# Pre-norm scales from sums gathered before the residual add, half of the residual update inside the state-space pipeline, and the direct term of that pipeline in its tables

## The chip, the cores and the metric

The kernel runs on one core of a Trainium2 chip. The metric is the device time of one execution in microseconds, the median of several runs. The engines are TensorE (PE; its weight loads PEld), VectorE (DVE), ScalarE (ACT), GpSimd (POOL) and SyncE (SP, which issues the DMA transfers).

## The reference

One inference step of a two-layer hybrid decoder over T = 576 positions (512 of a prompt, 8 sequences of 8 more) and a model width of 1024. Six sub-layers follow each other: feed-forward, S5 state-space mixer with GLU, feed-forward; feed-forward, multi-head latent attention, feed-forward. Each is wrapped in two norms:

```
x += w * RMSNorm_post(f(RMSNorm_pre(x)))        # w is 1/2 for the feed-forwards
rms_norm(x, g) = x * rsqrt(mean(x*x) + 1e-6) * g
swiglu(x)      = (silu(x @ w_gate) * (x @ w_up)) @ w_down          # inner width 2816
s5_mixer(u):   s_t = A s_(t-1) + B u_t (complex, 64 groups of 16 channels, 64 states)
               y = Re(C s) + d * u
               z = gelu(y) @ w_glu ; out = z[:1024] * sigmoid(z[1024:])
```

The other part of the reference, the attention with its projections and cache, is not touched by the change.

## The kernel before, in words

The residual stream X lies in SBUF as 8 blocks of 128 channels by 576 positions; the positions are worked in two halves of 288 (h = 0, 1). Matrix products run as three matmuls each (`mm3`, L156 to L158: high by high, high by low, low by high part), 128x288 per instruction. A block (m, h) below is one output block of 128 channels for one half.

RMS norms need sums over channels, that is over partitions. ScalarE squares each output block (L143), GpSimd adds the squares into ACC (L147), and TensorE multiplies ACC with a column of ones (`stats`, L103: four small matmuls for the four quarters of 72 positions of a half). VectorE makes the reciprocal root in nine small operations (L107 to L116, 72x4) and a diagonal matrix `rs_d` (L119); `spread` (L127) multiplies it with ones, so that every partition holds the scale of each position.

The end of a sub-layer is `tail`: the last two blocks of half 0, `stats` of half 0 (d0), block (6,1), then `post` for half 0 (L209: t = Y * g * scale; L211: X += t, partly on GpSimd; L153: split of X * g into high and low part, ACT and DVE), block (7,1), and two pending steps for half 1: its `stats` (d1) and its `post`. The pending steps are run inside the next sub-layer's `first_units`, which computes four output tiles of half 0 (96 matmuls), then of half 1 (96). After `post` the squares of the new X are taken and added once more (`squares`), and `first_units` asks for their `stats` and the two spreads into R, the scale of the pre-norm; R multiplies the products only at their evacuation (L313, L315), so the first products don't wait for it.

The state-space stage (`s_u`, `s_a`, `s_b`, ... ) is a software pipeline over k = 0 to 7 (128 channels each): transposes to time-major tiles (L692 or L700), transposes back (L711), input matmuls (L723), products with rotation tables `rt` (L728, L729), a scan with the decay factors (L737), products (L739 on POOL, L740 on DVE), output matmuls (L757, L760), the direct term d * u (L774), the GELU (L775 to L782) and the split (L153). Its tables (WV, RT, CA, KT, MD) are built during the first feed-forward, in pieces, and go through DRAM. Before the loop it takes squares of X half 1 on ScalarE, adds some on VectorE, and makes both scales.

The order of instructions on each engine is fixed when the kernel is built; each engine works its own list in order.

Of the kernel before, what the change touches and what calls it, by code (L numbers as in the profile page):

```python
# [17 lines left out]
T = 576  # L18
# [7 lines left out]
def build(nc, tc, a, subs=(0, 1, 2, 3, 4, 5)):  # L26
# [9 lines left out]
    with ctx:  # L36
# [40 lines left out]
        ACC = cst.tile([128, T], F32, name="ACC")  # L77
        GP = cst.tile([128, 6, 2, 8], F32, name="GP")
# [19 lines left out]
        def stats(accs, col=None, scale=1.0, eps=1e-6):  # L98

            src = psum()[:CP, :4]  # L100
            for i, z in enumerate(accs):
                for j in range(4):
                    P.matmul(src[:, j:j + 1], z[:, j * CP:j * CP + CP], ones[:, 0:1] if col is None else col,  # L103
                             start=i == 0 and j == 0, stop=i == len(accs) - 1 and j == 3)
            q, t, y = [cur["sm"].tile([CP, 4], F32, name=nm) for nm in ("rs_a", "rs_t", "rs_y")]

            V.tensor_scalar(q, src, eps, None, op0=OP.add)  # L107
# [8 lines left out]
            V.scalar_tensor_tensor(y, t, 5.0, y, op0=OP.add, op1=OP.mult)  # L116
            d = smt("rs_d")[:CP]
            state["y"] = y
# [3 lines left out]
            return d  # L122

# [8 lines left out]
        def sqacc(acc, src, first, scale=1.0, defer=False, ve=False, add=None):  # L132
# [6 lines left out]
            if first:  # L139
                A.activation(acc, src, AF.Square, scale=scale)  # L140
                return None
            sq = sqd.tile([128, H], F32, name="sqd") if defer else smt("sq")
            ins = A.activation(sq, src, AF.Square, scale=scale)  # L143
            if defer:
                state["sqd"] = ins
                return sq
            (add or G).tensor_tensor(acc, acc, sq, op=OP.add)  # L147
# [56 lines left out]

        def post(n, h, rs, nxt):
            last = None
            for k in range(8):
                t = smt("t1")
                V.scalar_tensor_tensor(t, Y[:, k, hs(h)], GP[:, n, 1, k:k + 1], rs, op0=OP.mult, op1=OP.mult)  # L209
                ve = k % 2 if nxt in (None, 1) else k % 4 == 0  # L210
                ins = (V if ve else G).tensor_tensor(X[:, k, hs(h)], X[:, k, hs(h)], t, op=OP.add)  # L211
                last = last if ve else ins
                if nxt is None:
                    if k % 2:
                        S.dma_start(a["o_y"][:, k - 1:k + 1, hs(h)], X[:, k - 1:k + 1, hs(h)])
                elif nxt != 1:
                    xsplit(nxt, h, k)
            if nxt == 1 and h == 1:
                state["add"] = last
                s5["D0"] = stats([ACC[:, hs(0)]]), state["y"]  # L220
                sqs = []
                for k in range(8):
                    sqs.append(s5["sq"].tile([128, H], F32, name="sq%d" % k))
                    A.activation(sqs[k], X[:, k, hs(h)], AF.Square)
                for x, y in ((4, 5), (6, 7), (4, 6)):
                    V.tensor_tensor(sqs[x], sqs[x], sqs[y], op=OP.add)
                s5["D1"] = stats(sqs[:5]), state["y"]
            elif h == 1:
                squares(h, nxt, last)
            return last  # L230

        def squares(h, nxt, last):
            if nxt is not None:
                with tc.issue_after(last.ins), tc.issue_after(state["sqd"].ins):
                    for k in range(8):
                        sqacc(ACC[:, hs(h)], X[:, k, hs(h)], k == 0, add=G)

# [1318 lines left out]
```

## Time and profile before

| | us |
|---|---|
| median of 3 runs | 2486.22 (2485.14 to 2488.54) |
| profiled execution, its time | 2486.95 |
| profiled execution, its span | 2485.2 |
| TensorE busy | 2381.8 (96%) |
| VectorE busy | 1281.5 (52%) |
| ScalarE busy | 873.6 (35%) |
| GpSimd busy | 556.1 (22%) |
| mean granted clock of TensorE | 0.978 of 2.4 GHz |

The span is what the profile sees, first to last instruction; the time has 1.8 us around it. Busy shares are averages over stages with different limits. In order of time the stages are: feed-forward (to 458), state-space start and loop (to 583), GLU (to about 690), two feed-forwards (to about 1560), attention (to about 2030), feed-forward.

### The profile page before, as it was taken

How to read it: one execution, taken by the hardware profiler on the slowest of the kernel's cores; microseconds unless marked ns; L12 is line 12 of the kernel's file. 1: busy time of each engine (PE TensorE's matmuls, PEld its weight loads, DVE VectorE, ACT ScalarE, POOL GpSimd, SP SyncE). 2: the span in 40 equal slices, each digit the busy share in tenths (PEclk: the TensorE clock that was granted, in tenths of full speed). 3: DMA queues.
4: the chain of work that ended last, by engine and by line, in shares of the span. 5: the costliest groups of instructions: out<-in, count | busy, mean ns of one | idle time of the engine just before them, and what ended most of it. 6: DMA issues, size and time to landing. Idle time of an engine off the chain costs nothing.

```text
span 2485.2 us, 44160 instructions
## 1 busy us (share of the span) xinstructions
PE 2381.8 (96%) x17610; PEld 2313.1 (93%) x17610; DVE 1281.5 (52%) x2647; ACT 873.6 (35%) x1807; POOL 556.1 (22%) x819
## 2 busy tenths in 40 slices
PE   7999999789989999998999999899999999999998
PEld 7999999679989999998999999798888898999997
DVE  7564565685464233347432433767777655423434
ACT  4222322353332222224222222434666653222221
POOL 3123535452231001124100112530000042100112
PEclk9999999799989999998999999999999999999999
DMA  3224343473212222222223222345555332222221
GB/s 126 86 86 146 126 130 118 125 188 97 77 60 86 71 92 86 75 88 68 80 67 101 86 70 76 114 114 178 169 173 179 130 104 69 75 74 99 86 71 63
DMA packets 114642, 254.89 MB, mean 103 GB/s; under 512 B 25122, under 2 KB 53539, under 8 KB 114179
## 3 DMA queue, kind: packets, MB, share of 16 engines
q1 hardware_dynamic: 114434, 252.06, 32.0%
q8 instruction: 139, 2.28, 0.4%
q14 instruction: 69, 0.56, 0.1%
HBM read 231.79 MB, written 22.59 MB: 102 GB/s over the span
## 4 chain that ended last, share of the span: by engine, by line
PE 68%; DVE 6%; ACT 2%; issue 1%; POOL 1%; DMA 1%; SPq 0%; ACTq 0%; DVEq 0%; POOLq 0%
PE ps L158 20%; PE ps L156 20%; PE ps L157 20%; PE ps L1331 2%; PE ps L1296 2%; DVE XHL L153 1%; DVE t L209 1%; POOL X L211 1%; PE ps L127 1%; PE ps L1237 1%; DVE wlo L151 1%; PE ps L1317 0%; PE ps L757 0%; PE ps L1225 0%; ACT Pm L1198 0%
## 5 line engine op out<-in xcount | busy, mean ns | idle before, releaser
L156 PE MATMUL ps<-XHL,whi 128*128 128x288 f32 x3344 | 1002.4, 300 | 20.4 <-ACT whi L151 12.9
L157 PE MATMUL ps<-XHL,whi 128*128 128x288 f32 x3344 | 998.7, 299 | 4.7 <-DVE XHL L153 4.7
L158 PE MATMUL ps<-XHL,wlo 128*128 128x288 f32 x3344 | 995.9, 298 | 1.4 <-DVE wlo L151 1.4
L156 PEld LDWEIGHTS ps<-XHL,whi 128*128 128x128 f32 x3344 | 638.2, 191 | 24.3 <-ACT whi L151 13.5
L157 PEld LDWEIGHTS ps<-XHL,whi 128*128 128x128 f32 x3344 | 639.0, 191 | 9.6 <-DVE XHL L153 7.4
L158 PEld LDWEIGHTS ps<-XHL,wlo 128*128 128x128 f32 x3344 | 637.9, 191 | 2.2 <-DVE wlo L151 2.0
L151 DVE TENSOR_TENSOR wlo<-raw,whi 128x1024 fp32r<-128x1024 f32 (+2 forms) x349 | 409.3, 1198 | 317.3 <-ACT whi L151 316.6
L151 ACT ACTIVATE whi<-raw 128x1024 fp32r<-128x1024 f32 (+2 forms) x349 | 321.6, 946 | 446.0 <-PE ps L157 378.2
L158 PE MATMUL ps<-HH,wlo 128*128 128x288 f32 x1408 | 415.8, 296 | 1.9 <-DVE wlo L151 1.9
L156 PE MATMUL ps<-HH,whi 128*128 128x288 f32 x1408 | 417.3, 296 | 0.0
L157 PE MATMUL ps<-HL,whi 128*128 128x288 f32 x1408 | 415.3, 295 | 0.0
L316 POOL TENSOR_TENSOR t<-t,t 128x288 f32<-128x288 f32 x176 | 143.1, 813 | 1113.2 <-DVE t L315 983.5
L158 PEld LDWEIGHTS ps<-HH,wlo 128*128 128x128 f32 x1408 | 265.2, 188 | 2.6 <-DVE wlo L151 2.6
L156 PEld LDWEIGHTS ps<-HH,whi 128*128 128x128 f32 x1408 | 265.3, 188 | 0.4
L157 PEld LDWEIGHTS ps<-HL,whi 128*128 128x128 f32 x1408 | 265.3, 188 | 0.2
L315 DVE TENSOR_TENSOR t<-ps,R 128x288 f32<-128x288 f32 x176 | 80.2, 456 | 331.3 <-PE ps L158 331.1
L147 POOL TENSOR_TENSOR ACC<-ACC,sq 128x288 f32<-128x288 f32 x137 | 138.3, 1010 | 391.2 <-ACT sq L143 387.0
L314 ACT ACTIVATE t<-t 128x288 f32<-128x288 f32 x176 | 77.9, 444 | 329.6 <-DVE t L313 313.2
L151 ACT ACTIVATE HH<-t 128x288 fp32r<-128x288 f32 x176 | 77.2, 439 | 249.0 <-POOL t L316 242.2
L151 DVE TENSOR_TENSOR HL<-t,HH 128x288 fp32r<-128x288 f32 x176 | 81.7, 465 | 125.2 <-ACT HH L151 124.8
L313 DVE TENSOR_TENSOR t<-ps,R 128x288 f32<-128x288 f32 x176 | 79.3, 450 | 53.8 <-PE ps L158 47.9
L369 DVE TENSOR_TENSOR Y<-ps,Y 128x288 f32<-128x288 f32 x64 | 29.2, 455 | 129.4 <-PE ps L158 129.4
(332 smaller groups left out, 2612.9 us busy)
## 6 DMA issues: line engine op xcount, KB each, us to landing
raw<-GU SPq DMA_DIRECT2D x176, 512.0 KB, 4.1
pgr<-PG SPq DMA_DIRECT2D x128, 320.0 KB, 3.5
raw<-DN SPq DMA_DIRECT2D x64, 512.0 KB, 3.5
raw<-DN SPq DMA_DIRECT2D x64, 192.0 KB, 3.4
raw<-GLU SPq DMA_DIRECT2D x16, 512.0 KB, 4.2
CAd<-s5w SPq DMA_DIRECT2D x8, 576.0 KB, 3.6
WVd<-s5w SPq DMA_DIRECT2D x8, 512.0 KB, 3.4
wv<-WVd SPq DMA_DIRECT2D x8, 512.0 KB, 5.8
```

The source lines that it names most:

```text
L147: (add or G).tensor_tensor(acc, acc, sq, op=OP.add)
L151: return A.activation(hi, src, AF.Copy), V.tensor_tensor(lo, src, hi.bitcast(F32), op=OP.subtract)
L156: P.matmul(o, wh, xh, start=st, stop=False)
L157: P.matmul(o, wh, xl, start=False, stop=False)
L158: P.matmul(o, wl, xh, start=False, stop=sp)
L313: V.tensor_tensor(t, pp[0], R[:, hs(h)], op=OP.mult)
L314: A.activation(s, t, AF.Silu)
L315: V.tensor_tensor(u, pp[1], R[:, hs(h)], op=OP.mult)
L316: g = G.tensor_tensor(u, u, s, op=OP.mult)
L369: ins = V.tensor_tensor(y, o, y, op=OP.add)
L1296: P.matmul(so, qb[:, cb], d["kv"][u][:, :, 256 + cb * 128:384 + cb * 128], start=cb == 0, stop=False)
L1331: P.matmul(o, d["pt"][:, c], d["kv"][i // 2][:, i % 2, 0:256], start=i == 0, stop=i == 3)
```

## The change

Three things are done.

- For every output block, three sums are gathered instead of one (`ymom`): of Y squared in ACC, of (Y g) X in R, of (Y g) squared in ACQ. ScalarE makes two squares, VectorE one product, GpSimd three adds. `mom_a` sends the six groups of small matmuls (two per sum) and makes the post-norm scale y; `mom_b` computes from the two other sums and the old sum of X squared, kept in SA, the sum of the new X squared: SA + y (2 sum(Y g X) + y sum((Y g)^2)), in six small VectorE operations, and with eight more the pre-norm scale and its diagonal. The squares of the new X after `post` go, and so do the `stats` in `first_units`. The spreads into R are written in `tail` and in its pending step.
- At the state-space stage `post` of half 1 is taken apart: `post1(k)` runs inside the pipeline's step for k, followed by a scaled copy of X on ScalarE. The pre-norm scale enters at the evacuation of the first transposes (eight ACT copies of 72x128 instead of two of 72x512).
- In the loop the direct term d * u is added to the KT table when that is built, the negated rotation and the scan's decay factors come as two more planes of RT (512 KB a step instead of 256), two additions and one product move from GpSimd to VectorE, and the GELU is rewritten with one VectorE instruction less per half.

```diff
+        def mom_a(h, SQ):
+            src = sums([[ACC[:, hs(h)], SQ[h][0]]])
+            bc = sums([[R[:, hs(h)], SQ[h][1]], [ACQ[:, hs(h)], SQ[h][2]]])
+            q = cur["sm"].tile([CP, 4], F32, name="rs_a")
+            V.tensor_scalar(q, src, 1e-6, None, op0=OP.add)
+            y = rsqrt(q)
+            return y, bc
+        def mom_b(h, y, bc):
+            m = cur["sm"].tile([CP, 4], F32, name="rs_m")
+            V.tensor_tensor(m, bc[:, 4:8], y, op=OP.mult)
+            V.scalar_tensor_tensor(m, bc[:, 0:4], 2.0, m, op0=OP.mult, op1=OP.add)
+            V.tensor_tensor(m, m, y, op=OP.mult)
+            V.tensor_tensor(SA[:, h], SA[:, h], m, op=OP.add)
+            V.tensor_scalar(SA[:, h], SA[:, h], 0.0, None, op0=OP.max)
+            q = cur["sm"].tile([CP, 4], F32, name="rs_ab")
+            V.tensor_scalar(q, SA[:, h], 1e-6, None, op0=OP.add)
+            y2 = rsqrt(q, "b")
+            return diag(y2, tag="b"), y2
+        def ymom(n, m, h, y, sc=1.0):
+            g = GP[:, n, 1, m:m + 1]
+            out = []
+            for i, acc in enumerate((ACC, R, ACQ)):
...
+                if i == 1:
+                    V.scalar_tensor_tensor(dst, y, g, X[:, m, hs(h)], op0=OP.mult, op1=OP.mult)
+                else:
+                    A.activation(dst, y, AF.Square, scale=g if i else sc)
+                if 0 < m < 7:
+                    G.tensor_tensor(acc[:, hs(h)], acc[:, hs(h)], dst, op=OP.add)
+                out.append(dst)
+            return out
...
-            d0 = stats([ACC[:, hs(0)], SQ[0]])
+            y0, bc0 = mom_a(0, SQ)
+            d0 = diag(y0)
             blk(mlast[0], 1)
...
-            last = post(n, 0, spread(d0), nxt)
+            post(n, 0, spread(d0), nxt)
             for m in mlast[1:]:
                 blk(m, 1)
-            squares(0, nxt, last)
-            d1 = []
-            state["pend"] = [lambda: d1.append(stats([ACC[:, hs(1)], SQ[1]])), lambda: post(n, 1, spread(d1[0]), nxt)]
+            if nxt == 1:
+                s5["D0"] = mom_b(0, y0, bc0)
...
+                    spread(d1, ACC[:, hs(1)])
+                    s5["post"] = lambda k: post1(n, 1, ACC[:, hs(1)], nxt, k)
...
+            if nxt is not None:
+                spread(mom_b(0, y0, bc0)[0], R[:, hs(0)])
+            z = {}
+            def norm1():
+                z["y"], z["bc"] = mom_a(1, SQ)
+                z["d"] = diag(z["y"])
+            def rest1():
+                post(n, 1, spread(z["d"]), nxt)
+                if nxt is not None:
+                    spread(mom_b(1, z["y"], z["bc"])[0], R[:, hs(1)])
+            state["pend"] = [norm1, rest1]
...
-            d0 = stats([ACC[:, hs(0)]])
...
-                        spread(d0, R[:, hs(0)])
...
-            spread(d1, R[:, hs(1)])
...
-                    V.scalar_tensor_tensor(u, X[:, k], GP[:, n, 0, k:k + 1], R, op0=OP.mult, op1=OP.mult)
+            def scaled(k):
+                s5["post"](k)
+                u = UN[k] = lp.tile([128, T], F32, name="un")
+                for h in range(2):
+                    A.activation(u[:, hs(h)], X[:, k, hs(h)], AF.Copy, scale=GP[:, n, 0, k:k + 1])
...
-                G.tensor_tensor(m1, Z, RT[:, 0:1].to_broadcast([128, 2, 4, 64]), op=OP.mult)
+                V.tensor_tensor(m1, Z, RT[:, 0:1].to_broadcast([128, 2, 4, 64]), op=OP.mult)
...
-                    V.tensor_scalar(w, sq, 0.044715, 1.0, op0=OP.mult, op1=OP.add)
-                    G.tensor_tensor(w, w, y, op=OP.mult)
+                    V.scalar_tensor_tensor(w, sq, 1 / 0.044715, y, op0=OP.add, op1=OP.mult)
```

What this does to the order of instructions is seen at two places, both at the boundary between the second and the third feed-forward. First TensorE's list at the end of block (7,1), the last product of the old sub-layer (HH, HL are its inputs, XHL those of the next sub-layer). Before:

```order
L156 MATMUL ps<-HH,whi 128x288
L157 MATMUL ps<-HL,whi 128x288
L158 MATMUL ps<-HH,wlo 128x288
L156 MATMUL ps<-XHL,whi 128x288
L157 MATMUL ps<-XHL,whi 128x288
L158 MATMUL ps<-XHL,wlo 128x288
```

And the same place of the changed kernel:

```order
L207 MATMUL ps<-HH,whi 128x288
L208 MATMUL ps<-HL,whi 128x288
L209 MATMUL ps<-HH,wlo 128x288
L181 MATMUL ps<-rs_d,ones 128x288
L207 MATMUL ps<-XHL,whi 128x288
L208 MATMUL ps<-XHL,whi 128x288
L209 MATMUL ps<-XHL,wlo 128x288
```

The spread of the pre-norm's half 0 (L181) now stands between the two; before, it came behind 71 of the first products, two stats groups, the spread of d1 and more products. In the changed kernel 12 first products follow it, then the six groups of half 1, 24 products, the spread of d1, 60 products, and the spread of the pre-norm's half 1 ahead of half 1's 96 products. At the boundaries into the attention and behind it the order is the same; into the second feed-forward that spread of half 0 stands there too, and the one of half 1 follows the spread of d1 by 30 products.

Second VectorE's list there, where that spread's diagonal is made (`rs_yb` is the pre-norm's reciprocal root, `rs_d` the diagonal, t and X belong to `post` of half 0). The changed kernel, first where the chain of `mom_b` meets `post`:

```order
L117 SCALAR_TENSOR_TENSOR rs_yb<-rs_tb,rs_yb 72x4
L420 TENSOR_TENSOR Y<-ps,Y 128x288
L118 SCALAR_TENSOR_TENSOR rs_tb<-rs_yb 72x4
L259 SCALAR_TENSOR_TENSOR t_12062<-Y,GP,ps 128x288
L170 SCALAR_TENSOR_TENSOR sq<-Y,GP,X 128x288
```

and, behind 15 further rows of `post` of half 0 and its weight splits, its end:

```order
L204 SCALAR_TENSOR_TENSOR XHL<-X,GP,XHL 128x288 x4
L420 TENSOR_TENSOR Y<-ps,Y 128x288
L119 TENSOR_TENSOR rs_tb<-rs_tb,rs_ab 72x4
L202 TENSOR_TENSOR wlo<-raw,whi 128x1024
L170 SCALAR_TENSOR_TENSOR t_12139<-Y,GP,X 128x288
L120 SCALAR_TENSOR_TENSOR rs_tb<-rs_tb 72x4
L202 TENSOR_TENSOR wlo<-raw,whi 128x1024
L121 SCALAR_TENSOR_TENSOR rs_yb<-rs_tb,rs_yb 72x4
L127 SCALAR_TENSOR_TENSOR rs_d<-ident,rs_yb 72x288
```

Eleven operations of `mom_b` stand in front of `post`, three and the diagonal behind it. Before, the rows at the end of that `post` were these:

```order
L153 SCALAR_TENSOR_TENSOR XHL<-X,GP,XHL 128x288 x4
L369 TENSOR_TENSOR Y<-ps,Y 128x288
L151 TENSOR_TENSOR wlo<-raw,whi 128x1024 x2
L107 TENSOR_SCALAR rs_a<-ps 72x4
L108 TENSOR_SCALAR rs_y<-rs_a 72x4
```

There the chain of d1, the post-norm scale of half 1, followed at once.

## Rows read from the trace of the kernel before

**Rows 1.** The page: busy time of each engine, share, instructions.

```profile
PE 2381.8 (96%) x17610; PEld 2313.1 (93%) x17610; DVE 1281.5 (52%) x2647; ACT 873.6 (35%) x1807; POOL 556.1 (22%) x819
```

**Rows 2.** What TensorE waited for: us in total, times, longest.

```profile
PE ps L127 <- DVE rs_d L119: 35.2, 13, 4.8
```

**Rows 3.** TensorE in order of time, the spreads: start, us, engine, line, operation.

```profile
1109.89 0.65 PE L127 MATMUL ps<-rs_d,ones 72*128 72x288 f32 x2
1130.26 1.14 PE L127 MATMUL ps<-rs_d,ones 72*128 72x288 f32 x2 [1.86 <-DVE rs_d L119]
1146.87 1.30 PE L127 MATMUL ps<-rs_d,ones 72*128 72x288 f32 x2 [3.70 <-DVE rs_d L119]
1159.38 0.65 PE L127 MATMUL ps<-rs_d,ones 72*128 72x288 f32 x2
```

**Rows 4.** TensorE in order of time: a sums group; block (7,1)'s end.

```profile
1104.28 0.29 PE L158 MATMUL ps<-HH,wlo 128*128 128x288 f32 x1
1104.41 0.62 PE L103 MATMUL ps<-ones,ACC 128*72 128x1 f32 x8
1104.89 0.38 PE L156 MATMUL ps<-HH,whi 128*128 128x288 f32 x1
1114.59 0.29 PE L158 MATMUL ps<-HH,wlo 128*128 128x288 f32 x1
```

**Rows 5.** VectorE in order of time, same boundary.

```profile
1106.69 0.16 DVE L107 TENSOR_SCALAR rs_a<-ps 72x4 f32<-72x4 f32 x1 [1.62 <-PE ps L103]
1108.43 0.45 DVE L119 SCALAR_TENSOR_TENSOR rs_d<-ident,rs_y 72x288 f32<-72x288 f32 x1
1110.09 0.46 DVE L369 TENSOR_TENSOR Y<-ps,Y 128x288 f32<-128x288 f32 x1 [1.20 <-PE ps L158]
1122.99 0.44 DVE L369 TENSOR_TENSOR Y<-ps,Y 128x288 f32<-128x288 f32 x1
1123.35 2.34 DVE L151 TENSOR_TENSOR wlo<-raw,whi 128x1024 fp32r<-128x1024 f32 x2
1131.43 0.94 DVE L209 SCALAR_TENSOR_TENSOR t<-Y,GP,ps 128x288 f32<-128x288 f32 x2 [1.23 <-PE ps L127]
1142.19 0.15 DVE L107 TENSOR_SCALAR rs_a<-ps 72x4 f32<-72x4 f32 x1
1145.79 0.94 DVE L119 SCALAR_TENSOR_TENSOR rs_d<-ident,rs_y 72x288 f32<-72x288 f32 x1
```

**Rows 6.** Stretches: length, each engine's busy time, granted clock, DMA share, GB/s.

```profile
1146.50:1149.00 2.50, 2.13 (x7) 1.87 (x8) 0.57 (x2) 0.41 (x1) 0.00 (x0) 0.50 0.00 0
1149.00:1151.50 2.50, 2.50 (x14) 2.50 (x14) 1.66 (x5) 1.22 (x3) 0.95 (x2) 0.61 0.00 0
```

**Rows 7.** State-space loop: a turn's stretch; VectorE's lines; one instruction.

```profile
513.00:523.00 10.00, 8.45 (x88) 6.98 (x88) 9.59 (x19) 5.81 (x17) 5.96 (x7) 1.00 0.92 234
L669 DVE SCALAR_TENSOR_TENSOR un<-X,GP,R 128x576 f32<-128x576 f32 x4 | 5.1, 1285 | 0.0
L774 DVE SCALAR_TENSOR_TENSOR t<-un,s5d,ps 128x288 f32<-128x288 f32 x10 | 4.7, 508 | 1.8 <-PE ps L772 1.8
L778 DVE TENSOR_SCALAR t<-sq 128x288 f32<-128x288 f32 x10 | 7.8, 782 | 1.1 <-ACT sq L775 1.1
L740 DVE TENSOR_TENSOR Y<-Y,rt 128x512 f32<-128x512 f32 x5 | 6.9, 1373 | 0.0
490.93 0.69 DVE L740 TENSOR_TENSOR Y<-Y,rt 128x512 f32<-128x512 f32 x1
```

**Rows 8.** GpSimd's adds in attention's output, then in the first feed-forward's end.

```profile
L147 POOL TENSOR_TENSOR ACC<-ACC,sq 128x288 f32<-128x288 f32 x12 | 11.1, 927 | 85.6 <-ACT sq L143 85.6
L147 POOL TENSOR_TENSOR ACC<-ACC,sq 128x288 f32<-128x288 f32 x12 | 16.4, 1367 | 36.8 <-ACT sq L143 36.8
```

**Rows 9.** TensorE in order of time, start of the state-space stage.

```profile
466.17 1.30 PE L127 MATMUL ps<-rs_d,ones 72*128 72x288 f32 x2 [4.75 <-DVE rs_d L119]
483.94 0.39 PE L723 MATMUL ps<-U,wv 128*64 128x72 f32 x2
```

More of the change, by code (lines that the diff above doesn't have):

```diff
@@ L95, in smt, with sums, rsqrt @@
             return cur["sm"].tile([128, w], dt, name=name, **(dict(bufs={"t1": 4, "sq": 3}[name]) if name in ("t1", "sq") else k))
-        def stats(accs, col=None, scale=1.0, eps=1e-6):
-            src = psum()[:CP, :4]
-            for i, z in enumerate(accs):
+        def sums(groups, col=None):
+            src = psum()[:CP, :4 * len(groups)]
+            lst = [(z, g) for i in range(max(map(len, groups))) for g, q in enumerate(groups) for z in q[i:i + 1]]
+            for i, (z, g) in enumerate(lst):
                 for j in range(4):
[L103 to L107, printed above, removed]
+                    P.matmul(src[:, 4 * g + j:4 * g + j + 1], z[:, j * CP:j * CP + CP], ones[:, 0:1] if col is None else col,
+                             start=i == 0 and j == 0, stop=i == len(lst) - 1 and j == 3)
+            return src
+        def rsqrt(q, tag="a"):
+            t, y = [cur["sm"].tile([CP, 4], F32, name=nm + tag) for nm in ("rs_t", "rs_y")]
             V.tensor_scalar(y.bitcast(I32), q.bitcast(I32), -0.5, float(0x5F1FFFF9), op0=OP.mult, op1=OP.add)
@@ L122, in stats @@
             return d
+        def stats(accs, col=None, scale=1.0, eps=1e-6, keep=None):
+            src = sums([accs], col)
+            q = cur["sm"].tile([CP, 4], F32, name="rs_a")
+            V.tensor_scalar(q, src, eps, None, op0=OP.add)
+            if keep is not None:
+                V.tensor_copy(SA[:, keep], src)
+            return diag(rsqrt(q), scale)
+        def mom_a(h, SQ):
+            src = sums([[ACC[:, hs(h)], SQ[h][0]]])
+            bc = sums([[R[:, hs(h)], SQ[h][1]], [ACQ[:, hs(h)], SQ[h][2]]])
+            q = cur["sm"].tile([CP, 4], F32, name="rs_a")
+            V.tensor_scalar(q, src, 1e-6, None, op0=OP.add)
[16 more added lines that the diff above has]
+            for i, acc in enumerate((ACC, R, ACQ)):
+                dst = acc[:, hs(h)] if m == 0 else (smt("t1") if i else sqd.tile([128, H], F32, name="sqd")) if m == 7 else smt("sq")
+                if i == 1:
[6 more added lines that the diff above has]
+            return out
         def spread(d, out=None):
@@ L130, in spread, with sqacc @@
             A.activation(out, pp, AF.Copy)
-        def sqacc(acc, src, first, scale=1.0, defer=False, ve=False, add=None):
+        def sqacc(acc, src, first, ve=False):
             if ve:
@@ L139, in sqacc @@
             if first:
-                A.activation(acc, src, AF.Square, scale=scale)
+                A.activation(acc, src, AF.Square)
                 return None
[L142 to L147, printed above, removed]
+            sq = smt("sq")
+            A.activation(sq, src, AF.Square)
+            G.tensor_tensor(acc, acc, sq, op=OP.add)
         def split(hi, lo, src, g=None):
@@ L203, in xsq, with post1 @@
                     sqacc(ACC[:, hs(h)], X[:, k, hs(h)], k == 0, ve=True)
+        def post1(n, h, rs, nxt, k):
+            t = smt("t1")
+            V.scalar_tensor_tensor(t, Y[:, k, hs(h)], GP[:, n, 1, k:k + 1], rs, op0=OP.mult, op1=OP.mult)
+            ve = k % 2 if nxt in (None, 1) else k % 4 == 0
+            (V if ve else G).tensor_tensor(X[:, k, hs(h)], X[:, k, hs(h)], t, op=OP.add)
+            if nxt is None:
+                if k % 2:
+                    S.dma_start(a["o_y"][:, k - 1:k + 1, hs(h)], X[:, k - 1:k + 1, hs(h)])
+            elif nxt != 1:
+                xsplit(nxt, h, k)
         def post(n, h, rs, nxt):
-            last = None
             for k in range(8):
[L208 to L236, printed above, removed]
+                post1(n, h, rs, nxt, k)
         def first(n, u):
@@ L808, in s5_mixer @@
                 if s == 0:
-                    for h in range(2):
-                        spread(DD[h][0], R[:, hs(h)])
-                    V.tensor_tensor(UN[0], UN[0], R, op=OP.mult)
                     s_u(1)
-                    with tc.issue_after(state["add"].ins) if "add" in state else nullcontext():
-                        zeros()
+                    zeros()
                 if rest:
@@ L1161, in mla @@
                 for h in range(2):
+                    if m == 2:
+                        for z in range(2):
+                            ymom(n, z, h, Y[:, z, hs(h)])
                     blk(m, h)
```

113 lines of the change are left out of this document (55 added, 58 removed).

## The prediction

> **What bounds the kernel now.** I read the page first: TensorE is busy 96% of the span, VectorE 52%, GpSimd 22% [rows 1]. So only time in which TensorE stands still or runs slowly can be won, and every added wait of TensorE costs in full. Then the waits of TensorE, costliest first: the spreads (line L127, a matmul of the diagonal `rs_d` with `ones`) wait 35.2 us for VectorE's `rs_d` [rows 2], more than for anything else. Then one boundary between sub-layers, second to third feed-forward. Four spreads mark it: post-norm half 0 at 1109.89, post-norm half 1 at 1130.26, pre-norm half 0 at 1146.87, pre-norm half 1 at 1159.38 [rows 3]. Two of them waited (1.86 and 3.70 us); the reader is to see that from the first to the last only 49.5 us pass, because the next sub-layer's first products fill TensorE while VectorE does `post`. Last the state-space loop: in one turn (513 to 523) VectorE is busy 9.59 of 10 us, TensorE 8.45, the DMA engines 0.92 [rows 7]. That stage alone is not held by TensorE.
>
> The sum is made against the profiled execution, 2486.95 us; the median of the runs, 2486.22, is 0.7 lower.
>
> **Extra sums on TensorE.** `mom_a` sends six groups of four small matmuls per half, two before. A group holds TensorE 0.48 us (1104.41 to 1104.89) [rows 4]. Four more groups of half 0 stand in front of its first spread and cost 1.9 us at each of six places. At the last tail nothing reads them: +1.9. At the other places they are in the sums below.
>
> **The boundaries: the wait moves.** The pre-norm scale of half 0 no longer needs a sum over the new X, so its spread could come early; but the order puts it right behind block (7,1), ahead of every first product of the next sub-layer, at three of the four boundaries. Its `rs_d` is built on VectorE only behind the whole of `post` half 0, a block's evacuation and two weight splits. From rows, with the first spread at 0: `post` half 0 ran from 1110.09 to 1122.99, that is until +13.1 [rows 5]. Ahead of it the change adds a small operation (0.2) and a product of 0.46; behind it stand the evacuation L369 (0.36), a split of 1.15, another product (0.45), the second split (1.15), three small operations (0.2 each) and `rs_d` (0.45): 4.2. The diagonal is ready near +17.5; +16 if GpSimd lets VectorE run free, +18.5 if not (the same nine small operations took 1.7 us from 1106.69 to 1108.43, and 3.6 from 1142.19 to 1145.79, where `rs_d` took 0.94) [rows 5].
>
> TensorE ends block (7,1) at +4.5 and has nothing else in the order: it stands still some 13 us, where it now works with short breaks. After a 3.70 us wait the granted clock was 0.50, the 1.2 GHz level, and 0.61 over the next window, which is 0.55 us of it at 2.4 GHz: back some 4.1 us after the restart [rows 6]. A matmul of 288 columns starts every 0.13 us at the full clock (1104.28 to 1104.41) [rows 4], so 0.26 at half. From +17.5: 12 matmuls at half clock (3.1), one group (1.0), five groups at full (2.4), 24 matmuls (3.1), spread of half 1 at +27.1 (now +20.4). `post` half 1 begins 1.2 later and takes 10.8 (1131.43 to 1142.19) [rows 5]; two small operations, two evacuations and `rs_d` add 1.8: the last spread goes at +40.9. TensorE finished half 0's other 60 products at +35.3 and waits 5.6 us, drops to 1.2 GHz again, and needs 14.6 us for 96 products (15 in the first 4 us, 81 at full): +55.5. Now this point is the last spread plus six products, +50.7. The loss is 4.8, with the groups 6.7; from the two bounds (and `post` half 1 up to 0.9 shorter) 4.3 to 7.7. The boundary into latent attention and the one into the last feed-forward have the same order. From GLU into the second feed-forward the half-0 diagonal comes early, but half 1's stands behind `post` half 1, four evacuations and a split that waits for ScalarE and GpSimd, with only 30 products ahead of the spread; the same working gives a wait of 12 and, groups included, a loss of 5 (3.5 to 6.5). Three times 6.7 and 5: **+25**, bounds +16 to +30.
>
> That rests on the order holding on the chip. The evacuation L369 shows it: its block's last matmul began at 1114.59, and it ran at 1122.99, in its place behind `post` [rows 4, 5]. [...] Were it free to overtake, the diagonal would be ready at +3, no boundary would lose more than its groups (1.9), and the whole sum would be 17 us lower.
>
> **More work for GpSimd.** Three adds per output block instead of one. In the attention's output stretch an add took 0.93 us [rows 8]; three make 2.8 of a block's 3.15 (24 matmuls), nearly full but not over. In the first feed-forward's tail an add took 1.37 [rows 8], beside the table building; what comes late there may delay a few weight loads: **+1**, bounds 0 to 4. The extra squares on ScalarE (35% busy) and the product on VectorE lie beside TensorE in all other blocks: 0; without that cover 16 blocks by 0.45 a sub-layer.
>
> **Start of the state-space stage.** Now: spread at 466.17, then stats over eight new squares and two more chains, first L723 at 483.94 [rows 9]. After: the scale y2 follows the post chain at once. Spread 466.17, copy of it 0.6, `post1` for k=0 1.4 with GpSimd's add, scaled copy 0.4, eight transposes at half clock 1.2, eight small evacuations 2.2, second transposes and copies 1.7, issue gaps 1: first L723 near 475. Minus 1.9 for the groups in front: **−7**, bounds −4 to −9. All eight `post1` stand on VectorE before its first product of the loop, which bounds it at the upper end.
>
> **The loop.** Off VectorE go the scaled product L669 (1.29 a turn), two L774 (0.51) and two L778 (0.78): 3.9 [rows 7]. On come two additions of 256 (0.4), one product of 512 at 0.69 (490.93, GpSimd idle) and two fused products in place of L778 (0.45): 2.4, and L740 falls from 1.37 toward 0.69 as GpSimd's partner instruction is gone [rows 7]. VectorE then needs some 7.5 us, so TensorE's 8.45 bounds the turn, if the data come: DMA is already 0.92 busy in this turn and the decay table doubles (256 KB more, a tenth of a turn's 2.34 MB). I take 8.7 for 10, seven turns: **−9**; bounds 0 (DMA-bound in every turn) and −11 (8.45).
>
> [...]
>
> **Sum.** +25 +1.9 +1 −7 −9 = +12: 2498.9 against the profiled 2486.95, 2498.2 against the median.
>
> **Rivals.** 0.2% (5 us) is about what a measurement tells from no change.
> - *Cheap boundaries, same time.* Chains run free, each boundary at its lower bound: +16 +1.9 +0 −7 −9 = +2, 2488. For it: squares after `post` are gone from GpSimd, which alternated with the chains. Against: 13 us of standing still cannot be free.
> - *The gains prevail, faster.* The state-space stage at its bounds (−9, −11) with cheap boundaries: 16 + 1.9 − 20 = −2; if VectorE, which then shares less with GpSimd, ends each `post` another 1.5 us sooner, −8: 2478. It decides once a boundary loses under 3.3 us. For it: TensorE has no more breaks in the rest of `first_units`. Against: its clock drops twice in each.
> - *GpSimd saturates, slower still.* If an add takes more than 1.05 us, three exceed a block's 3.15. At 1.37 they need 4.1, 0.95 too much in 12 blocks: 11 us late at the sums of the attention's output, +12 +11 = +23, 2509.
> - *The doubled table makes the loop DMA-bound at 10 us a turn*: +12 +9 = +21, 2507. For it: the 0.92 [rows 7]; against: TensorE and VectorE, not a transfer, filled that turn.
>
> **Chances.** Forecast with its own bounds (2491 to 2506) 0.5, same time 0.22, faster 0.16, GpSimd or DMA 0.12. Part of the forecast's lower edge lies within 0.2%: slower 0.59, same 0.24, faster 0.17. The range 2478 to 2509 leaves about 0.1 on either side.
>
> **What would show it.** After: the pre-norm spread of half 0 waits 11 to 14 us at three boundaries, half 1's 5 (12 into the second feed-forward), each followed by 1.2 GHz windows; span from first spread to the last first product some 55 us. First L723 8 to 12 us after the spread of post-norm half 1 (17.8 now); a turn of 8.4 to 9 us with VectorE under 8. I am wrong if those spreads wait under 8 us, if `rs_d` appears before `post` ends, if the turn stays at 10, or if TensorE waits for GpSimd's sums before the spreads.

## The result and the profile after

The changed kernel takes 2548.98 us (median of 4 runs, 2543.43 to 2556.42), the kernel before 2486.63 in the same number of runs: a ratio of 1.0251 [1.0237, 1.0265]. It is slower, as forecast, but by 62 us and not by 12, and far outside the range. The profiled execution took 2549.25 us, with a span of 2547.5 and a mean granted clock of 0.967 (0.978 before).

First the page's busy times and, from the view of waits, what TensorE waited for (us in total, times, longest). They answer to [rows 1, 2].

```profile
PE 2410.2 (95%) x17878; PEld 2346.2 (92%) x17878; DVE 1312.9 (52%) x2799; ACT 897.3 (35%) x1880; POOL 601.8 (24%) x866
PE ps L181 <- DVE rs_d L127: 67.2, 12, 13.4
PE ps L207 <- ACT whi L202: 18.2, 6, 8.8
PE ps L760 <- ACT TT L750: 9.0, 7, 3.7
PE ps L806 <- DMA CKb<-CAd: 4.1, 1, 4.1
PE ps L106 <- POOL ACC L174: 4.0, 1, 4.0
```

The spreads wait 32 us longer than before: half of the loss. TensorE's busy time rose by 28.4 us too. The 268 matmuls more are nearly all sums, 34 groups, 16 us at the 0.48 us a group of [rows 4] (the trace counts each of a group's four matmuls twice, hence x8); the rest points to work done at a lower clock, and the mean clock did fall, from 0.978 to 0.967.

**Where the 62 us arose.** The same product (the n-th matmul of 288 columns) was looked up in both traces; how much later it starts after the change, at the end of each stage, is what the stages so far have cost. Differences of that, from one trace of each kernel, give:

| stage | forecast, us | measured, us |
|---|---|---|
| first feed-forward (GpSimd's work) | +1 | +15.7 |
| sums behind it, state-space start, loop | -7 -9 | -10.1 |
| boundary into the second feed-forward | +5 | +8.2 |
| second to third feed-forward | +6.7 | +12.4 |
| third feed-forward to attention | +6.7 | +13.2 |
| attention to the last feed-forward | +6.7 | +19.2 |
| end | +1.9 | +3.7 |
| sum | +12 | +62.3 |

**One boundary, TensorE in order of time.** The same boundary as in [rows 3], second to third feed-forward: sums groups (L106) and spreads (L181).

```profile
1117.95 0.62 PE L106 MATMUL ps<-ones,ACC 128*72 128x1 f32 x8
1122.46 1.05 PE L106 MATMUL ps<-ones,t 128*72 128x1 f32 x8
1128.67 0.65 PE L181 MATMUL ps<-rs_d,ones 72*128 72x288 f32 x2
1147.12 1.33 PE L181 MATMUL ps<-rs_d,ones 72*128 72x288 f32 x2 [13.41 <-DVE rs_d L127]
1159.44 0.65 PE L181 MATMUL ps<-rs_d,ones 72*128 72x288 f32 x2
1171.30 0.72 PE L181 MATMUL ps<-rs_d,ones 72*128 72x288 f32 x2 [3.31 <-DVE rs_d L127]
```

The second spread, that of the pre-norm's half 0, waits 13.41 us, the fourth 3.31. But look also at the first two times: from the first sums group to the first spread it is now 10.7 us (1117.95 to 1128.67), and was 5.5 (1104.41 to 1109.89 [rows 3, 4]). Four groups of 0.48 us should have added 1.9; 5.2 came.

**The clock there.** Stretches of the same boundary: length, busy time of PE, PEld, DVE, ACT and POOL, then granted clock, DMA share, GB/s.

```profile
1118.00:1120.50 2.50, 2.50 (x33) 2.50 (x32) 0.97 (x2) 0.87 (x2) 0.00 (x0) 1.00 0.00 0
1120.50:1123.00 2.50, 2.50 (x26) 2.50 (x24) 1.55 (x10) 0.00 (x0) 0.00 (x0) 0.67 0.00 0
1123.00:1125.50 2.50, 2.50 (x14) 2.50 (x14) 1.93 (x11) 0.00 (x0) 0.00 (x0) 0.50 0.02 7
1125.50:1128.00 2.50, 2.50 (x12) 2.50 (x12) 0.00 (x0) 0.00 (x0) 0.00 (x0) 0.50 0.00 0
1149.50:1152.00 2.50, 2.50 (x16) 2.50 (x16) 0.00 (x0) 0.00 (x0) 0.00 (x0) 0.50 0.16 62
1152.00:1154.50 2.50, 2.50 (x40) 2.50 (x40) 1.44 (x10) 0.00 (x0) 0.00 (x0) 0.98 0.00 0
1154.50:1157.00 2.50, 2.50 (x18) 2.50 (x18) 2.12 (x12) 0.00 (x0) 0.00 (x0) 0.70 0.03 7
```

In and behind the six groups of half 0 the granted clock falls to 0.50, which the prediction calls the 1.2 GHz level (a product of 288 columns starts every 0.24 us, 1123.75 to 1128.07, ahead of the groups every 0.13), although TensorE is busy in every stretch, 2.50 of 2.50 us; it falls a second time behind the groups of half 1 (0.70), after it had come back from the long wait (0.98).

**VectorE, same boundary**, in order of time, answers to [rows 5].

```profile
1128.87 0.46 DVE L420 TENSOR_TENSOR Y<-ps,Y 128x288 f32<-128x288 f32 x1 [3.42 <-PE ps L209]
1140.53 2.77 DVE L204 SCALAR_TENSOR_TENSOR XHL<-X,GP,XHL 128x288 fp32r<-128x288 f32 x4
1143.22 0.44 DVE L420 TENSOR_TENSOR Y<-ps,Y 128x288 f32<-128x288 f32 x1
1146.44 0.15 DVE L121 SCALAR_TENSOR_TENSOR rs_yb<-rs_tb,rs_yb 72x4 f32<-72x4 f32 x1
1146.62 0.45 DVE L127 SCALAR_TENSOR_TENSOR rs_d<-ident,rs_yb 72x288 f32<-72x288 f32 x1
```

`post` ends at 1143.3, 14.6 after the first spread; the evacuation, two weight splits and the rest of the chain follow, and the diagonal comes at the very end, as the order said.

**First feed-forward.** Four engines in order of time, 419 to 431. L608 is the building of the rotation tables; L612 makes the new negated plane; L170 and L174 are the new product and the adds; L202 splits weights.

```profile
419.01 0.32 POOL L608 TENSOR_TENSOR s5w<-s5w 128x64 f32<-128x64 f32 x1
420.90 1.04 DVE L170 SCALAR_TENSOR_TENSOR sq<-Y,GP,X 128x288 f32<-128x288 f32 x1 [7.39 <-POOL R L174]
425.04 0.45 POOL L608 TENSOR_TENSOR s5w<-s5w 128x128 f32<-128x128 f32 x1
425.53 0.42 ACT L612 ACTIVATE s5w<-s5w 128x256 f32<-128x256 f32 x1 [12.97 <-POOL s5w L608]
426.61 1.04 ACT L202 ACTIVATE whi<-raw 128x1024 fp32r<-128x1024 f32 x1
427.70 0.40 PE L207 MATMUL ps<-HH,whi 128*128 128x288 f32 x1 [2.71 <-ACT whi L202]
427.93 1.03 DVE L170 SCALAR_TENSOR_TENSOR sq<-Y,GP,X 128x288 f32<-128x288 f32 x1 [5.63 <-POOL R L174]
428.89 1.81 DVE L202 TENSOR_TENSOR wlo<-raw,whi 128x1024 fp32r<-128x1024 f32 x1
430.75 0.61 PE L209 MATMUL ps<-HH,wlo 128*128 128x288 f32 x1 [2.52 <-DVE wlo L202]
```

Read it backwards from TensorE. At 427.70 it waits for a weight split on ScalarE; that stood behind the plane copy, which had waited 12.97 us for GpSimd's chain. At 430.75 it waits for a split on VectorE; that stood behind the new product, which had waited for a buffer whose last reader is an add on GpSimd.

**State-space stage**, TensorE in order of time, and the stretch of one turn; they answer to [rows 7, 9].

```profile
483.88 1.33 PE L181 MATMUL ps<-rs_d,ones 72*128 72x288 f32 x2 [0.89 <-DVE rs_d L127]
494.03 1.23 PE L772 MATMUL ps<-U,wv 128*64 128x72 f32 x16
522.82 0.72 PE L760 MATMUL ps<-ident,TT 72*128 72x72 f32 x8 [0.67 <-ACT TT L750]
532.10 0.72 PE L760 MATMUL ps<-ident,TT 72*128 72x72 f32 x8 [0.68 <-ACT TT L750]
532.00:541.30 9.30, 8.60 (x88) 6.96 (x88) 7.44 (x18) 6.84 (x24) 0.95 (x2) 1.00 0.78 225
```

From the spread of the post-norm's half 1 to the first input product it is 10.2 us now, 17.8 before. A turn takes 9.28 (522.82 to 532.10), not 8.7.

### The profile page after: what moved, and what is told of

The parts are those of the page before. It is cut to its first block, busy times and chain, and to the rows that moved or that the text cites. A ratio compares the mean times of both kernels' runs of the same rounds, so it can differ in the third digit from the quotient of the medians.

```text
span 2547.5 us, 44935 instructions
## 1 busy us (share of the span) xinstructions
PE 2410.2 (95%) x17878; PEld 2346.2 (92%) x17878; DVE 1312.9 (52%) x2799; ACT 897.3 (35%) x1880; POOL 601.8 (24%) x866
## 5 line engine op out<-in xcount | busy, mean ns | idle before, releaser
L207 PEld LDWEIGHTS ps<-XHL,whi 128*128 128x128 f32 x3344 | 637.8, 191 | 16.9 <-ACT whi L202 15.4
L202 DVE TENSOR_TENSOR wlo<-raw,whi 128x1024 fp32r<-128x1024 f32 (+2 forms) x349 | 412.8, 1207 | 280.0 <-ACT whi L202 279.4
L202 ACT ACTIVATE whi<-raw 128x1024 fp32r<-128x1024 f32 (+2 forms) x349 | 321.7, 946 | 415.4 <-PE ps L208 355.0
L202 ACT ACTIVATE HH<-t 128x288 fp32r<-128x288 f32 x176 | 77.1, 438 | 237.5 <-POOL t L367 230.7
L174 POOL TENSOR_TENSOR ACC<-ACC,sq 128x288 f32<-128x288 f32 x72 | 86.0, 1195 | 286.0 <-ACT sq L172 286.0
L202 DVE TENSOR_TENSOR HL<-t,HH 128x288 fp32r<-128x288 f32 x176 | 80.7, 459 | 137.7 <-ACT HH L202 137.2
```

Of the source, the lines that this page charges most:

```text
L174: G.tensor_tensor(acc[:, hs(h)], acc[:, hs(h)], dst, op=OP.add)
L202: return A.activation(hi, src, AF.Copy), V.tensor_tensor(lo, src, hi.bitcast(F32), op=OP.subtract)
L207: P.matmul(o, wh, xh, start=st, stop=False)
```

## The experiments

Two theories stood after the result. One: the spreads, placed behind `post`'s diagonal, cost the boundaries; the rest is small. The other: the extra sums and GpSimd's work cost most, wherever the spreads stand. Ratios are to the kernel before, measured again beside each run, with their 95% interval; "drift" is the lateness of the same product, as in the table. A drift is that of one trace, and the places where the clock falls differ from trace to trace, some 3 us each (e4, e10: 5.2 us at a place or 2.1): a difference of that size between two drifts tells nothing alone.

**e1, late spreads.** The spreads into R go back behind the first products; all else is as changed.

```diff
-                spread(mom_b(0, y0, bc0)[0], R[:, hs(0)])
+                state["r0"] = mom_b(0, y0, bc0)[0]
...
+                        spread(state.pop("r0"), R[:, hs(0)])
                         for v in range(2):
                             evac(v, 0, pp[v])
+            spread(state.pop("r1"), R[:, hs(1)])
```

> The changed kernel with the two pre-norm spreads moved behind the first products of the next sub-layer, where they stood before; sums, chains and adds unchanged. If the place of the spreads costs the time (theory): the waits of 11 to 13 us at four boundaries and of 3.3 us behind them go, the extra sums and the first feed-forward's loss stay; 25 to 30 us less than the changed kernel, near 2520. If TensorE then waits as long for something else, for VectorE's chains or the residual blocks (rival): less than 8 us gained, above 2540.

Measured: 2493.09 us, 1.0020 [1.0007, 1.0034]. Moving two spreads at each boundary gives back 56 of the 62 us, twice the 25 to 30 expected. In the view of waits, and in order of time at the same boundary:

```profile
PE ps L181 <- DVE rs_d L127: 7.1, 5, 3.0
1141.26 0.65 PE L181 MATMUL ps<-rs_d,ones 72*128 72x288 f32 x2
1145.20 0.65 PE L181 MATMUL ps<-rs_d,ones 72*128 72x288 f32 x2
```

No pre-norm spread of this boundary waits; the drift goes from 1.8 to -0.2 over it, and from -0.2 to -8.7 over the next, so that these boundaries are as short as before or shorter, groups included. Over all four the drift falls by 6 us, where it rose by 53 as changed. Three losses stay: 17.6 in the first feed-forward with the sums at its end, 8.5 behind the attention, and 5.1 at the last sums. So the first theory holds for the boundaries, and the second for what stays.

**e2, planes and adds.** On the changed kernel: the plane copy from ScalarE to GpSimd, two of three adds of the first feed-forward to VectorE.

```diff
-                    G.tensor_tensor(acc[:, hs(h)], acc[:, hs(h)], dst, op=OP.add)
+                    (V if n == 0 and i else G).tensor_tensor(acc[:, hs(h)], acc[:, hs(h)], dst, op=OP.add)
...
-                            A.activation(NR[:, 0], RT[:, 1], AF.Copy, scale=-1.0)
+                            G.tensor_scalar(NR[:, 0], RT[:, 1], -1.0, None, op0=OP.mult)
```

> The changed kernel with the negated plane of the rotation table made by GpSimd instead of ScalarE, and the adds of the two further sums of the first feed-forward made by VectorE instead of GpSimd. If ScalarE and VectorE stand behind GpSimd there and the weight splits queue behind them (theory): the first feed-forward is back within 3 us of its old length plus the 2 us of the extra sums, 12 to 15 us less than the changed kernel, near 2535. If the weight loads themselves come late, from the table's doubled transfers (rival): less than 4 us gained.

Measured: 2557.64 us, 1.0288 [1.0271, 1.0305]; the drift at the stage's end is 19.1 (17.8 as changed). No gain, where 12 to 15 us were expected. One add left on GpSimd is enough: ScalarE's squares now wait for it, and weight splits stand behind them (view of waits, ScalarE):

```profile
ACT sq L172 <- POOL ACC L174: 19.5, 6, 7.2
```

This trace also shows what the boundary costs without the first fall of the clock. Its edits don't touch the boundaries; first sums group and the two spreads of half 0, second to third feed-forward:

```profile
1117.41 0.62 PE L106 MATMUL ps<-ones,ACC 128*72 128x1 f32 x8
1125.05 0.65 PE L181 MATMUL ps<-rs_d,ones 72*128 72x288 f32 x2
1143.51 1.33 PE L181 MATMUL ps<-rs_d,ones 72*128 72x288 f32 x2 [13.41 <-DVE rs_d L127]
```

The wait is the same 13.41 us, but from the sums to the first spread it is 7.6 us instead of 10.7, with a granted clock of 1.00, and the boundary costs 8.7 us instead of 12.4; the next one, where the clock stays up behind these sums too, 7.8 instead of 13.2.

**e3, moments once.** The gathered sums are kept only ahead of the state-space stage; the other boundaries and the end are written as before (`stats`, `squares`).

```diff
-            y0, bc0 = mom_a(0, SQ)
-            d0 = diag(y0)
+            if nxt == 1:
+                y0, bc0 = mom_a(0, SQ)
+                d0 = diag(y0)
+            else:
+                d0 = stats([ACC[:, hs(0)], SQ[0]])
```

> The changed kernel with gathered sums at the first boundary only; at the other four the pre-norms are taken from squares of the new X as before the change. By the two traces the last five sub-layers lost 54 us outside the state-space stage. If that is all due to the gathered sums (theory): 2549 - 54, near 2495, and every stage from GLU on is as long as before within 1 us. If a part of it comes from elsewhere, say other buffers or code (rival): 2505 or more.

Measured: 2489.47 us, 1.0005 [0.9996, 1.0015]. The drift is 15.8 behind the first feed-forward, 3.3 behind the loop and between 2.4 and 3.4 in the middle of every sub-layer from there to the end: all boundaries run as before. So the state-space gain of 12.5 is real and paid away before it begins.

**e4, unread sums.** The kernel before, with 16 small matmuls (four groups) more in a row ahead of each two-part `stats`, twelve places; nothing reads them.

```diff
+            if len(accs) == 2:
+                for i in range(16):
+                    P.matmul(src[:, 4 + i:5 + i], accs[0][:, i % 4 * CP:i % 4 * CP + CP], ones[:, 0:1], start=i == 0, stop=False)
```

> The kernel before the change with four more groups of small matmuls (unread) in front of each tail's sums, sixteen matmuls in a row, 12 places. If such narrow matmuls cost only their own 0.48 us a group (rival): 12 us at the six places of half 0, and up to 12 at half 1, so 2498 to 2510. If TensorE's clock also falls to 1.2 GHz in or behind them without any pause of TensorE, as it did at 1121 us of the changed kernel (theory): 3 us more at each place where that happens, 2505 to 2535, and stretches of granted clock 0.50 right behind the groups in which TensorE is busy throughout.

Measured: 2517.65 us, 1.0121 [1.0104, 1.0138]. Of the six places of half 0 three cost 2.1 us, the sums' own time, and three 5.2, where the clock falls behind them; those of half 1 cost between 0 and 3.2 each. That is the size that e1 could not give: four groups more are worth up to 5.2, with nothing else changed.

**e5, late spreads and first feed-forward.** e1, and for the first feed-forward all three adds on VectorE, the plane copy on GpSimd, and the stores of the RT tables moved to the end of a piece of table building.

```diff
+                    (V if n == 0 else G).tensor_tensor(acc[:, hs(h)], acc[:, hs(h)], dst, op=OP.add)
...
-                            S.dma_start(s5["RT"][k, :, 0:2], RT)
-                            S.dma_start(s5["RT"][k, :, 2:4], NR)
+                            S_["NR"] = NR
...
+                    S.dma_start(s5["RT"][k, :, 0:2], RT)
+                    S.dma_start(s5["RT"][k, :, 2:4], S_["NR"])
```

> The late spreads of the first experiment, and in the first feed-forward all three adds of each output block on VectorE, the negated plane on GpSimd, and the rotation table's stores moved on SyncE's queue to the end of their chunk, behind the weight loads they stood in front of. If the loss of 17.6 us there came from engines and a queue that stand behind GpSimd's rotation chain (theory): it falls to the extra sums, 2 to 5 us, and the time to near 2480. If the added work itself fills ScalarE or VectorE (rival): 12 us or more of the loss stay, 2487 or more.

Measured: 2478.79 us, 0.9974 [0.9951, 0.9996]. The two new planes are stored after their place was written anew, so this kernel and the next compute the state-space output from other numbers; their work is the same. The drift is -0.9 at 245 us (5.7 as changed) and 1.8 ahead of the sums (15.7): the loss of this stage was GpSimd's and the stores', together; the stores were not moved alone.

**e6, and the attention's output.** e5, with one of three adds per block in the attention's output on VectorE.

```diff
+                    (V if n == 0 or n == 4 and i == 1 else G).tensor_tensor(acc[:, hs(h)], acc[:, hs(h)], dst, op=OP.add)
```

> The kernel before this one, with one of the three adds of each block in the attention's output on VectorE instead of GpSimd. If GpSimd, nearly full there, makes the sums late (theory: TensorE waited 4.0 us for ACC at 2065 of the changed kernel): 3 to 5 us less than its sibling, near 2476. If that wait is hidden or moves to the chain (rival): the same time as its sibling within 1.5 us.

Measured: 2476.21 us, 0.9953 [0.9939, 0.9968]. Over this boundary the drift falls by 1.0, where it rose by 6.0 in e5, and TensorE's wait for ACC falls from 4.2 to 1.3 us. The medians differ by 2.6 only, but e9 and e12, with the same add moved, show -1.2 and -0.3 over this boundary, and e1 and e8, without it, 8.5 and 5.7. Three adds were too much for GpSimd there.

**e7, chain first.** The changed kernel, spreads early, with `mom_b` and its diagonal written ahead of `post`.

```diff
+            r0 = mom_b(0, y0, bc0)
...
-                spread(mom_b(0, y0, bc0)[0], R[:, hs(0)])
+                spread(r0[0], R[:, hs(0)])
```

> The changed kernel with the spreads where the change put them, right behind the last block, but with the pre-norm's chain and diagonal written ahead of the residual blocks, so that VectorE makes them first. If only the late diagonal makes the early spread dear (theory): the waits of 11 to 13 us fall below 2 us, and the time comes near that of the late spreads, 2490 to 2500. If the chain, put first, delays the residual blocks by as much as it saves (rival): waits for their products instead, above 2510.

Measured: 2519.90 us, 1.0140 [1.0123, 1.0157]. In order of time at the same boundary, the two pre-norm spreads:

```profile
1125.23 0.75 PE L181 MATMUL ps<-rs_d,ones 72*128 72x288 f32 x2
1151.65 1.33 PE L181 MATMUL ps<-rs_d,ones 72*128 72x288 f32 x2 [5.69 <-DVE rs_d L127]
```

Half 0's wait is gone, which shows that `post` ahead of the diagonal made it, and the four boundaries cost 14 us in place of 53. Half 1's wait is longer (3.31 as changed): its spread comes 8.9 us behind the post-norm's spread of half 1 instead of 11.9, but TensorE has only 19 products for that time instead of 60. e1 stays 27 us better: the time is the rival's, above 2510, not the theory's.

**e8, late spreads and adds only.** e1 with all three adds of the first feed-forward on VectorE; the plane copy stays on ScalarE, the stores where they were.

```diff
+                    (V if n == 0 else G).tensor_tensor(acc[:, hs(h)], acc[:, hs(h)], dst, op=OP.add)
```

> The late spreads of the first experiment, and of the first feed-forward's edits only the adds: all three of each output block on VectorE; plane and stores as in the change. If two things stood behind GpSimd (theory): the loss near 425 us (8 us, blocks whose squares wait for a free buffer) goes, the 5.7 us between 190 and 245 (table stores ahead of weight loads) stay; near 2485. If the adds are all of it (rival 1): near 2479. If the stores are all of it (rival 2): no gain, 2493.

Measured: 2499.44 us, 1.0042 [1.0028, 1.0057]; drift 16.9 at the stage's end, no gain over e1, where 8 us were expected. View of waits, ScalarE:

```profile
ACT s5w L614 <- POOL s5w L610: 38.8, 8, 10.8
```

The plane copy still waits for GpSimd and holds ScalarE's weight splits. With e2, where one add was left on GpSimd: neither of the two cures the stage while the other stays, since either one blocks a queue in which weights are split.

**e9, combined.** e6 with the stores one piece later, so that the tables are whole, and without the two extra sums in the last sub-layer, which nothing reads.

```diff
-            for i, acc in enumerate((ACC, R, ACQ)):
+            for i, acc in enumerate((ACC, R, ACQ) if n < 5 else (ACC,)):
...
+                out = [load] + [rot(i) for i in range(6)] + last + [store]
```

> Late spreads, the first feed-forward's adds on VectorE, plane on GpSimd and the table's stores one piece later, one of three adds of the attention's output on VectorE, and no second and third sum in the last sub-layer, where nothing reads them. If the costs found so far add up (theory): the 2476 of the sixth run less 2 to 3 us at the end, 2470 to 2477, faster than before the change by 0.4 to 0.6%. If the later stores, still ahead of some weight loads, keep part of the first feed-forward's loss (rival): 2478 to 2483.

Measured: 2476.15 us, 0.9956 [0.9943, 0.9970], within the 2470 to 2477 of the theory; but the drift ahead of the sums is 5.7, from one wait of TensorE:

```profile
433.47 0.61 PE L209 MATMUL ps<-HH,wlo 128*128 128x288 f32 x1 [5.62 <-DVE wlo L202]
```

**e10 and e11, unread sums in a row or apart.** The kernel before with four groups more at six places, ahead of half 0's sums only: 16 matmuls in a row in e10, the same 24 groups one per output block in e11.

```diff
+        def unread(c):
+            src = psum()[:CP, :4 * c]
+            for i in range(4 * c):
+                P.matmul(src[:, i:i + 1], ones[:, i % 4 * 8:i % 4 * 8 + CP], ones[:, 0:1], start=i == 0, stop=i == 4 * c - 1)
...
+            unread(4)
```

> The kernel before the change with four unread groups, sixteen narrow matmuls in one row, at six places. Own time alone (rival): 2.05 us a place, 12.3 in all, 2499. With a fall of TensorE's clock at some of the places, as in the fourth run, where places cost either 2.1 or 5.2 us (theory): 3.1 us more at each, 2502 to 2518.

> The same 24 groups as in its sibling, but one by one, each behind a whole block of products. If it is the row of narrow matmuls that lets the clock fall (theory): no fall, 12 to 13 us, 2499. If any narrow matmul near the end of a sub-layer does it (rival): as much as its sibling, within 2 us.

Measured: e10 2510.14 us, 1.0096 [1.0081, 1.0110]; e11 2499.85 us, 1.0049 [1.0035, 1.0064]. The same work costs 10 us more in rows. Stretches of e10 at the boundary into the second feed-forward (columns as above; the row of 16 runs from 665.90 to 668.08), then one of e11 there:

```profile
665.50:668.00 2.50, 2.50 (x38) 2.50 (x37) 0.45 (x1) 0.44 (x1) 0.00 (x0) 1.00 0.00 0
668.00:670.50 2.50, 2.50 (x21) 2.50 (x20) 0.00 (x0) 0.00 (x0) 0.00 (x0) 0.61 0.03 7
670.50:673.00 2.50, 2.50 (x14) 2.50 (x14) 1.61 (x10) 0.00 (x0) 0.00 (x0) 0.50 0.00 0
673.00:675.50 2.50, 2.50 (x12) 2.50 (x12) 0.27 (x1) 0.00 (x0) 0.00 (x0) 0.53 0.00 0
```

```profile
665.00:670.00 5.00, 5.00 (x51) 5.00 (x50) 2.34 (x11) 0.44 (x1) 0.00 (x0) 1.00 0.01 3
```

TensorE never stops in either; e10 loses 1.3 us in each stretch at 0.5. In e10 the clock falls so at three of six places (5.2, 5.2 and 4.8 us), at three it doesn't (2.1). In e11 it falls at none of the six.

**e12, combined, planes at the end.** e9 with the planes made and stored at the end of a piece, and half of the eight small copies of a turn (L750 of the changed kernel) on VectorE.

```diff
+                        if j < 2 or k == 0:
+                            A.activation(TT[:, :, 7 - 4 * h - j], pj, AF.Copy, scale=DD[h][1][:, j:j + 1])
+                        else:
+                            V.tensor_scalar(TT[:, :, 7 - 4 * h - j], pj, DD[h][1][:, j:j + 1], None, op0=OP.mult)
```

> The ninth run's kernel with the two added planes made and the table's stores issued at the end of each chunk, and with half of the small evacuations of the loop's first transposes (from the second step on) on VectorE instead of ScalarE. If SyncE's queue behind GpSimd holds the rest of the first feed-forward's loss (theory): that stage is 4 to 5 us shorter than in the ninth run. If ScalarE's eight small evacuations bound the loop's turn, 9.28 us in the changed kernel (theory): a turn of 8.6 to 8.9, 2 to 4 us less. Together near 2469. If VectorE, in turn, makes the products late (rival for the loop): a turn of 9.2 us or more, and near 2472.

Measured: 2474.14 us, 0.9939 [0.9926, 0.9953], 0.6% faster than the kernel before; from e9 it can't be told apart. The 2469 expected was not reached. In the first feed-forward the drift ahead of the sums is -0.5 (5.7 in e9), behind them 3.2. The copies were the wrong half of the edit, as the rival said: the waits of TensorE moved to VectorE and grew, a turn takes 9.85 us (517.24 to 527.09, in order of time) instead of 9.28.

```profile
517.24 0.69 PE L765 MATMUL ps<-ident,TT 72*128 72x72 f32 x8 [1.28 <-DVE TT L756]
527.09 0.69 PE L765 MATMUL ps<-ident,TT 72*128 72x72 f32 x8 [1.28 <-DVE TT L756]
```

## Why the prediction came out as it did

**The sign and its mechanism were right.** The pre-norm spread of half 0 waits 13.41 us, 13.41 and 13.13 at the three boundaries named (some 13 forecast), 10.97 into the second feed-forward (12), and half 1's 3.3 (5.6). The diagonal stands where VectorE's list has it: it ran at 1146.62, behind `post`, which ended at 1143.3. e1 and e7 show the cause by moving the spread and by moving the chain. How much hangs on it was not seen: without these waits the boundaries come out 6 us shorter than before (e1).

**The step that failed is the size of "The boundaries: the wait moves": 25 forecast, 53 measured (8.2 + 12.4 + 13.2 + 19.2).** That is 28 of the 50 us missed; 15 lie in the first feed-forward, 6 in the gains, 2 at the end. Two terms of it were too small, and a rival came on top.
- *A sums group was taken at 0.48 us, its own time.* Where the clock falls, four more cost 5.2 instead of 1.9, as at the second-to-third boundary and the next; e2, with the clock up there, has them 4 to 5 us cheaper. e10 and e11 show it with TensorE busy throughout. I read the clock only behind waits [rows 6], and took a busy TensorE for a fast one.
- *The clock after the restart.* It did come back some 5 us after the 13 us wait, near the 4.1 that was said; but half 1's sums stand there, and behind them it fell again: from the pre-norm's spread to half 1's it took 12.3 us (1147.12 to 1159.44) instead of 9.6. From there to the last spread it was 11.9 instead of 13.8, so the two misses partly cancel; the 96 products behind it took 14.9, as worked out (14.6).
- *GpSimd at the attention's output* was a rival (0.12 with the one on DMA) with the mark "an add over 1.05 us": the sums there waited 4.0 us for it (first fence), which the prediction had named as a sign of being wrong, and the traces of e6 and e5 differ by 7.0 us over this boundary for one add in three. The adds of before took 0.93 us with long rests between them [rows 8]; the 32 in the same stretch after the change took 1.00 (ACC), 1.07 (R) and 1.10 (ACQ), 1.05 on average. The mark itself was too high: from the first add (2031.55) to TensorE's being ready for the sums (2061.85) there are 30.3 us, and 31 adds had to be through, 0.98 each.

**"More work for GpSimd" failed too: +1 forecast, bounds 0 to 4; 15.7 measured in the first feed-forward.** I asked what the sums would wait for. What waited was VectorE and ScalarE: three adds a block go through a ring of three buffers, so one late add holds the product L170, and the plane copy L612 waits for the rotation chain. Behind both stand weight splits, and TensorE waits for those. e2 and e8 show that curing one of them keeps the loss, e5 and e12 that both cured, with the stores moved, remove it. Of the first 5.7 us (190 to 245) it was not separated which of the stores and the others it needs.

**The state-space start: right.** First input product 10.15 us after the spread (8 to 12 forecast, 17.8 before).

**The end: half of it.** 1.9 were forecast for half 0's four groups; half 1's four stand at the end as well, and 3.7 came.

**The loop: half.** 0.75 us a turn instead of 1.3; from its first input product into the GLU 4.4 us of the 9 were gained. VectorE fell to 7.44 as forecast (7.5): the product of 512 that took 1.37 us on average [rows 7] takes 0.68 with GpSimd 0.95 of 9.3 us busy. One row was misread: at 490.93 GpSimd was not idle. In the trace of before:

```profile
491.03 1.72 POOL L739 TENSOR_TENSOR Y<-Y,rt 128x512 f32<-128x512 f32 x1 [1.44 <-issue]
510.12 0.94 POOL L779 TENSOR_TENSOR t<-t,t 128x288 f32<-128x288 f32 x1 [0.25 <-DVE t L778]
510.33 1.28 DVE L740 TENSOR_TENSOR Y<-Y,rt 128x512 f32<-128x512 f32 x1
```

The two L740 that took 0.69 began 0.10 us before GpSimd's L739; the six that took 1.27 to 1.78 began with a GpSimd instruction under way. So 0.69 was the right price for another reason than the one given. But TensorE waits 0.67 a turn for ScalarE's eight small copies, which I had costed at nothing, and 4.1 once for a table's transfer. DMA, the rival, was 0.78 busy: but for that one wait it didn't bind. e12 tells that VectorE has no room for these copies where its list has them.

**Of the rivals** "GpSimd saturates" was there as well as the forecast, not in its place. "The gains prevail" is what e12 makes of the change, by other edits than the rival had in mind: the gain in the state-space stage with cheap boundaries and cheap adds, 13.7 us faster than before.

## What to carry to other kernels

Place a matmul that needs a small result behind work that is ready, not where its result is first defined: two moved spreads were worth 56 us. When work is added to an engine that is little used, don't compare its sum with the time that there is; ask whose buffers it holds, and what stands in those engines' queues behind the instruction that waits. And a row of one-column matmuls has to be priced with the clock behind it, 5.2, 5.2 and 4.8 us at three of six places here instead of 2.1 (e10); one group at a time among wide products cost only its own time, 0.52 us a group (e11).

## What the runs showed of the hardware

The granted clock fell to 0.50 with TensorE unbroken: behind 16 matmuls of one column and the sums after them, at 2.50 of 2.50 us busy (e10: 0.61, 0.50, 0.53). It fell at three of six places of e10 and at none of the six of e11, where the same groups stood one by one among wide products; at this case's second-to-third boundary the same row left it at 1.00 in e10 and in e4. What decides between the two is not settled: the same instructions in the same order at that boundary gave 0.50 in the changed kernel and 1.00 in e2.

A VectorE product of two SBUF inputs of 128x512 took 0.68 to 0.69 us with GpSimd at rest (the changed kernel) or when it began 0.10 us before GpSimd's, and 1.27 to 1.78 when a GpSimd instruction was already running (the kernel before). What makes it longer then, no run shows.
